# Two-layer encoder trunk: pools laid out anew, first weights ahead of the parameters, layer 1's loads spread over each head, layer 1's head outputs kept in SBUF

## The chip, the core and the metric

The kernel runs on one core of a Trainium2 chip. The metric is the device time of one launch in microseconds. The engines are PE (TensorE, matmuls), DVE (VectorE), ACT (ScalarE), POOL (GpSimd) and SP (SyncE), which here issues every DMA in one queue, in order.

## The reference

The input is x, 2048 tokens by 1024, in float32. There are two layers:

```
layer 0: h = rms_norm(x); proj = h @ W_in          (1024 x 3328)
  mixer A: 8 query heads on 2 KV heads, rotary, window of 3 chunks of 64, a learned sink
  mixer B: 8 heads, own chunk + 8 before, relative-position bias
  x1 = x + concat(A * silu(gate_a), B * silu(gate_b)) @ W_out
layer 1: h = rms_norm(x1); proj = h @ W_in         (1024 x 4096)
  mixer C, 8 heads: a = softmax(q1 k1) - lam * softmax(q2 k2), causal by chunk of 64
  o = rms_norm(a @ v) * (1 - lambda_init)
  out = x1 + (o * silu(gate)) @ W_out
```

## The kernel before

All matmul operands are split into a high and a low part (`...H`, `...L`), and a product is three matmuls (hi·hi and two cross terms, `mm3`, L214 to L216). The tokens are four blocks (b = 0 to 3) of 512, each four tiles (j) of 128. There are four stages, one after the other:

- **p0** (`_project`, layer 0). `hidden(b)` loads four x tiles (`xt`), normalizes them and transposes them into `p0h`. `weights` loads a group of columns in four pieces of 512 KB (`ws`, L297), splits each into `wH` (ACT copy, L303) and `wL` (POOL subtraction, L304). Each group is multiplied with two blocks of tokens. `tables()` loads the small parameters, multiplies out the rotary tables, and comes between the two blocks of `hidden`.
- **m** (`_mix0`): both attention mixers of layer 0 and its output projection (`mom`). `qd` holds a head's high query part (three buffers), `ql` the low part (two buffers).
- **p1** (`_project`, layer 1), in two halves of two blocks: the q, k and v columns, written to DRAM.
- **c** (`_mix1`): mixer C. Heads run block by block from b = 3 down to 0, eight heads to a block. `scores(h, b)` works through j and, in each j, through the two maps m and the key chunks z of 512: two matmuls into `cS` (L878, L879), row maximum on DVE (`cnm`, L882), exponential on ACT (`cP`, L885). `values(h, b)` transposes the weights (`ctr`, L925), splits them into `cptH` (ACT) and `cptL` (DVE), and multiplies them with v into `cO` (L932 to L934). `side()` brings other matmul work between: the gates of all blocks (`cG`, 288 steps, weights `cwH`, `cwL`) and then the output projections (`com`).

The order of the work in c is set by `pace`, which lets the values trail the scores by `LAG1` units and takes as many side steps as the table `STAGES1` gives for the units done. Instructions are then put on the engines by a scheduler that simulates the program; on the chip each engine, and SP's queue of DMAs, runs its list in order. A tile waits until the tile that had its buffer is done with, and the first tiles of a new stage's pool wait for what lay at that place in the stage before: pools are stacked in the order in which they are made.

In c before the change, `load(h, i, K, V)` loads for head h and key chunk i the four pieces of K (L1002, L1003) and then V (L1009), all ahead of the head's scores, and q after that (L859, L860). A head's output `o` is gated in `rest()`; for b = 1 and 2 it is stored to a DRAM tensor `o`, and `fetch(b)` reads it back later and splits it into `y` for the output projection.

Of the kernel before, what the change touches and what calls it, by code (L numbers as in the profile page):

```python
# [85 lines left out]
class Trunk:  # L86
# [6 lines left out]
    STAGES1 = ((0, 0), (600, 288), (780, 360), (1000, 440), (1088, 520))  # L93
# [130 lines left out]
    def _project(self, es, layer):  # L224
# [68 lines left out]
        def weights(c0, width, W=W):  # L293
            wH, wL = [], []
            for kh in range(4):
                ws = st.tile([P, 2, 512], F32, tag="ws", name=n + "ws")
                nc.sync.dma_start(  # L297
                    ws[:, :, :width],
                    W[kh * 256:(kh + 1) * 256, c0:c0 + width].rearrange("(k p) c -> p k c", p=P),
                )  # L300
                for k in range(2):
                    h, l = weight_tiles()
                    nc.scalar.activation(h[:, :width], ws[:, k, :width], AF.Copy)  # L303
                    nc.gpsimd.tensor_tensor(l[:, :width], ws[:, k, :width], f32(h[:, :width]), ALU.subtract)  # L304
                    wH.append(h)
                    wL.append(l)
            return wH, wL

        def hidden(b):
            hH, hL = hidden_tile("H", b), hidden_tile("L", b)  # L310
            for j in range(NTB):
# [8 lines left out]
                for q in range(2):  # L320
# [8 lines left out]
                    nc.vector.tensor_tensor(oL, ps3, f32(oH), ALU.subtract)  # L329
            if layer == 1 and b < NB - 1:  # L330
# [78 lines left out]
        for half in range(2):  # L409
            blocks = (2 * half, 2 * half + 1)  # L410
            h = [hidden(blocks[0])]
# [4 lines left out]
            for gi, (kind, c0, width, o) in enumerate(groups):  # L416
                w = weights(c0, width)
# [87 lines left out]
    def _mix0(self, es):  # L505
# [18 lines left out]
        def load_q(H, L, h, b, res):  # L524
# [6 lines left out]
            ql = ld.tile([P, BLK], F32R, tag="ql", name=n + "ql")  # L531
# [203 lines left out]
        def projected(b):  # L735
# [3 lines left out]
            for j, c in units:  # L739
# [87 lines left out]
    def _mix1(self, es):  # L827
        nc, tc, a, s = self.nc, self.tc, self.a, self.s1
        n = "c"
        pool = lambda nm, bufs, **kw: es.enter_context(tc.tile_pool(name=n + nm, bufs=bufs, **kw))  # L830
        ot = pool("ot", 4)
        sm = pool("sm", 8)
        ld = pool("ld", 2)
        yp = pool("y", 2 * KT)
        vp = pool("v", 4)
        pp = pool("pp", 19)
        kp = pool("kp", 4)
        sb = pool("sb", 2)
# [12 lines left out]
        def scores(h, b, K, res):  # L851

            tok = slice(b * BLK, (b + 1) * BLK)
            qd = ld.tile([P, 2, BLK], F32R, tag="qd", name=n + "qd")
            ql = ld.tile([P, 2, BLK], F32R, tag="ql", name=n + "ql")
            for m in range(2):
                r = slice(m * HD, (m + 1) * HD)
                for part, q in (("qH", qd), ("qL", ql)):
                    nc.sync.dma_start(f32(q[0:HD, m, :]), s[part][h, r, tok])  # L859
                    nc.sync.dma_start(f32(q[HD:P, m, :]), s[part][h, r, tok])  # L860
            us = res["u"] = []
            for j in range(NTB):
# [9 lines left out]
                for m in range(2):  # L872
                    chunks = []
                    for z, (c, ce) in enumerate(cuts):
                        wd = ce - c
                        ps = pS.tile([P, 512], F32, tag="S", name=n + "S")[:, :wd]
                        kt = K[z][m]
# [5 lines left out]
                        chunks.append((sb if m else pp).tile([P, 512], F32, tag=f"P{m}", name=n + f"P{m}", bufs=6 if m else None))  # L883
                        acc = la[:, m, z:z + 1] if nb > 1 else l[:, m:m + 1]
                        nc.scalar.activation(chunks[z][:, :wd], ps, AF.Exp, bias=nm[:, m, z:z + 1], accum_out=acc)  # L885
                        yield wd / 256
# [28 lines left out]
        def values(h, b, V, res):  # L915
# [3 lines left out]
            for kt in range(nkt):  # L919
# [6 lines left out]
                H = sb.tile([P, 512], F32R, tag="ptH", name=n + "ptH", bufs=3)  # L926
                L = sb.tile([P, 512], F32R, tag="ptL", name=n + "ptL", bufs=3)
# [3 lines left out]
                vH, vL = (v[:, kk:kk + P] for v in V[kt // 4])  # L931
                mm(o, vH, H[:, :wd], start=(kt == 0), stop=False, skip_group_check=True)  # L932
                mm(o, vH, L[:, :wd], start=False, stop=False, skip_group_check=True)  # L933
                mm(o, vL, H[:, :wd], start=False, stop=(kt == nkt - 1), skip_group_check=True)  # L934
# [8 lines left out]
        def gate(h, b, O):  # L943

            rows, tok = slice(h * P, (h + 1) * P), slice(b * BLK, (b + 1) * BLK)
            g = sb.tile([P, BLK], F32, tag="g", name=n + "gg")
# [10 lines left out]
            def rest():  # L957
# [10 lines left out]
                ended.add((h, b))  # L968
# [3 lines left out]
        def y_tile(b):  # L972
            if b:
                return yp.tile([P, BLK], F32R, tag="y", name=n + "y")
            pl, tag = late.pop(0)
            return pl.tile([P, BLK], F32R, tag=tag, name=n + "y" + tag, bufs=3 if pl is ld else None)

        def split(h, b, o):
            yH, yL = y_tile(b), y_tile(b)
            nc.scalar.activation(yH, o, AF.Copy)  # L980
            nc.gpsimd.tensor_tensor(yL, o, f32(yH), ALU.subtract)
            y[b][h] = yH, yL

        def fetch(b):

            for h in range(8):
                while (h, b) not in ended:
                    yield 0
                if b < NB - 1:
                    o = ot.tile([P, BLK], F32, tag="ot", name=n + "oy")  # L990
                    nc.sync.dma_start(o, s["o"][h * P:(h + 1) * P, b * BLK:(b + 1) * BLK])
                    split(h, b, o)
                    yield 1

        def load(h, i, K, V):

            tok = slice(i * BLK, (i + 1) * BLK)
            ks = []
            for m in range(2):
                k = kp.tile([P, BLK], F32R, tag=f"k{m}", name=n + f"k{m}")  # L1000
                r, o = slice(m * HD, (m + 1) * HD), slice((1 - m) * HD, (2 - m) * HD)
                nc.sync.dma_start(f32(k[r, :]), s["kH"][h, r, tok])  # L1002
                nc.sync.dma_start(f32(k[o, :]), s["kL"][h, r, tok])  # L1003
                ks.append(k)
            K.append(ks)
# [7 lines left out]
            V.append(vs)  # L1013

        room = self.last_hidden
        ended = set()
        late = [(ld, "wH"), (ld, "wL")] * 3 + [(kp, "k0"), (kp, "k1"), (vp, "vH"), (vp, "vL")] * 2 + [(pp, "P0")] * 2
# [5 lines left out]
        def gates():  # L1023

            for b in reversed(range(NB)):
                tok = slice(b * BLK, (b + 1) * BLK)
                for c in range(8):
                    ps = pG.tile([P, BLK], F32, tag="G", name=n + "G")
                    for k in range(KT):
                        if k % 4 == 0:  # L1030
                            w = []
                            for part in "HL":
                                t = ld.tile([P, 4, P], F32R, tag="w" + part, name=n + "w" + part, bufs=3)
# [47 lines left out]
        def projected_last():  # L1081

            w = [(room[0][:, k, :], room[1][:, k, :]) for k in range(KT)], []
            tags = [(ld, "qd"), (ld, "ql")] * 2, [(sb, "P1")] * 6 + [(kp, "k0"), (kp, "k1")]
# [4 lines left out]
            for i in range(4):  # L1089
                pairs.append([  # L1090
                    pl.tile([P, BLK], F32R, tag=tag, name=n + "w" + tag, bufs=6 if tag == "P1" else None)
# [4 lines left out]
            for c, w in ((1, w[0]), (0, pairs)):  # L1096
                tiles = [out_begin(0, j, c) for j in range(NTB)]
                for k in range(KT):
                    while (k, 0) not in ended:
                        yield 0  # L1100
# [9 lines left out]
        def heads():  # L1110
            for b in reversed(range(NB)):
                at[0] = b
                for h in range(8):
                    K, V = [], []
                    for i in range(b + 1):
                        load(h, i, K, V)
                    res = {}
                    yield from scores(h, b, K, res)
                    queue.append(values(h, b, V, res))
            queue.append(leave())  # L1120
# [6 lines left out]
        def side():  # L1127
            yield from gates()
            for b in (3, 2, 1):
                yield from fetch(b)  # L1130
# [51 lines left out]
```

## Time and profile before

| | |
|---|---|
| median of three runs | 2928.43 us (2926.35 to 2938.07) |
| profiled execution: time, span | 2935.29 us, 2933.5 us |
| mean granted TensorE clock | 0.972 |
| PE, DVE, ACT, POOL busy | 2726.8, 1937.4, 1595.9, 1610.5 us |
| moved by DMA | 555.83 MB, mean 189 GB/s |
| stages (first matmuls of each) | p0 from 0, m from about 610, p1 from about 1204, c from 1804 us |

The granted clock is told in shares of the full rate. PE is busy 93% of the span, so its idle time is 206 us in all; where an engine waits, the profile names what it waited for last.

### The profile page before, as it was taken

Reading aid. Unit: us, or ns where it says so; the run is one execution under the profiler, and the core shown is the slowest. Engines: PE = TensorE matmul, PEld = TensorE weight load, DVE = VectorE, ACT = ScalarE, POOL = GpSimd, SP = SyncE. Lnnn points to the kernel's source line nnn. Section 1 sums busy time; section 2 is a strip of 40 time slices with the busy share of each in tenths; the row PEclk is TensorE's granted clock in tenths of the full one; section 3 lists DMA queues with packets and bytes.
Section 4 is the critical chain, followed back from the end, with each engine's and each line's share of the span. In section 5 each row is a group of like instructions: output and inputs, shape, how many; then the busy total and the mean of one; then the engine's idle time right before and its main releaser. Section 6 shows DMA issues by size and latency. Waiting matters only on the chain.

```text
span 2933.5 us, 45206 instructions
## 1 busy us (share of the span) xinstructions
PE 2726.8 (93%) x13704; PEld 2243.6 (76%) x13704; DVE 1937.4 (66%) x4685; ACT 1595.9 (54%) x4135; POOL 1610.5 (55%) x1968
## 2 busy tenths in 40 slices
PE   7999999998999999999999997889999999898898
PEld 5878888886887887777888885767777777677667
DVE  7752385256788885698548832656657888888742
ACT  4443543367676664334343322657657777777752
POOL 3541251246344443367646631767767778888851
PEclk9999999999999999999999998999999999999999
DMA  4673343649887764567884454585867777668863
GB/s 149 224 249 128 116 144 122 196 145 245 218 205 172 191 176 123 193 209 258 271 288 129 130 176 148 165 233 164 248 180 217 203 226 216 181 182 220 209 216 115
DMA packets 408866, 555.83 MB, mean 189 GB/s; under 512 B 47152, under 2 KB 187184, under 8 KB 408624
## 3 DMA queue, kind: packets, MB, share of 16 engines
q1 hardware_dynamic: 408624, 552.96, 64.1%
q8 instruction: 109, 1.79, 0.3%
q14 instruction: 133, 1.09, 0.1%
HBM read 388.18 MB, written 164.63 MB: 188 GB/s over the span
## 4 chain that ended last, share of the span: by engine, by line
PE 64%; DMA 11%; DVE 11%; ACT 4%; issue 2%; POOL 2%; SPq 1%; DVEq 0%; ACTq 0%; POOLq 0%
PE p1mm L216 4%; PE p1mm L214 4%; PE p1mm L215 4%; PE cS L878 3%; PE cS L879 3%; PE ctr L925 3%; PE p0mm L214 2%; PE p0mm L215 2%; PE p0mm L216 2%; PE cG L214 2%; PE cG L215 2%; PE cG L216 2%; PE cO L933 2%; PE mom L214 2%; PE com L214 2%
## 5 line engine op out<-in xcount | busy, mean ns | idle before, releaser
L885 ACT ACTIVATE cP<-cS,cnm 128x512 f32<-128x512 f32 (+3 forms) x640 | 398.4, 629 | 183.0 <-DVE cnm L882 104.3
L882 DVE TENSOR_REDUCE cnm<-cS 128x1 f32<-128x512 f32 (+3 forms) x640 | 373.6, 600 | 105.9 <-PE cS L879 100.6
L878 PE MATMUL cS<-ck,cqd 128*128 128x512 f32 (+3 forms) x640 | 265.7, 420 | 56.4 <-ACT cP L885 19.7
L304 POOL TENSOR_TENSOR p0wL<-p0ws,p0wH 128x512 fp32r<-128x512 f32 (+1 forms) x128 | 155.5, 1246 | 274.3 <-ACT p0wH L303 264.9
L214 PE MATMUL p1mm<-p1wH,p1hH 128*128 128x512 f32 x768 | 301.8, 394 | 0.8 <-ACT p1wH L303 0.8
L215 PE MATMUL p1mm<-p1wL,p1hH 128*128 128x512 f32 x768 | 301.8, 393 | 0.4 <-POOL p1wL L304 0.4
L216 PE MATMUL p1mm<-p1wH,p1hL 128*128 128x512 f32 x768 | 301.9, 394 | 0.0
L912 POOL TENSOR_TENSOR cP<-cP,cP 128x512 f32<-128x512 f32 (+3 forms) x256 | 284.7, 1132 | 0.4
L304 POOL TENSOR_TENSOR p1wL<-p1ws,p1wH 128x512 fp32r<-128x512 f32 x128 | 167.9, 1331 | 137.1 <-ACT p1wH L303 117.6
L214 PE MATMUL p0mm<-p0wH,p0hH 128*128 128x512 f32 (+1 forms) x640 | 238.1, 375 | 3.4 <-ACT p0vt L454 2.9
L879 PE MATMUL cS<-ck,cql 128*128 128x512 f32 (+3 forms) x640 | 238.1, 377 | 2.9 <-DMA cql<-qL 2.9
L216 PE MATMUL p0mm<-p0wH,p0hL 128*128 128x512 f32 (+1 forms) x640 | 238.2, 373 | 0.1
L215 PE MATMUL p0mm<-p0wL,p0hH 128*128 128x512 f32 (+1 forms) x640 | 238.2, 373 | 0.0
L929 DVE TENSOR_TENSOR cptL<-ctr,cptH 128x512 fp32r<-128x512 f32 (+1 forms) x320 | 190.5, 599 | 62.9 <-ACT cptH L928 62.1
L928 ACT ACTIVATE cptH<-ctr 128x512 fp32r<-128x512 f32 (+1 forms) x320 | 169.9, 539 | 64.8 <-PE ctr L925 63.5
L878 PEld LDWEIGHTS cS<-ck,cqd 128*128 128x128 f32 x640 | 124.6, 195 | 98.4 <-ACT cP L885 45.7
L906 POOL TENSOR_SCALAR cP<-cP,ccs 128x512 f32<-128x512 f32 (+3 forms) x288 | 188.9, 672 | 0.0
L925 PE MATMUL ctr<-ident,cP 128*128 128x128 f32 x1088 | 175.5, 277 | 0.6 <-POOL cP L912 0.3
L898 POOL TENSOR_SCALAR ccs<-ce,crl 128x4 f32<-128x4 f32 (+2 forms) x96 | 26.9, 280 | 270.1 <-ACT cP L885 130.1
L911 POOL TENSOR_SCALAR cP<-cP,ccs 128x512 f32<-128x512 f32 (+3 forms) x256 | 173.6, 691 | 0.0
L215 PEld LDWEIGHTS p1mm<-p1wL,p1hH 128*128 128x128 f32 x768 | 144.8, 189 | 29.8 <-POOL p1wL L304 0.8
L214 PEld LDWEIGHTS p1mm<-p1wH,p1hH 128*128 128x128 f32 x768 | 144.7, 189 | 29.7 <-ACT p1wH L303 1.0
(325 smaller groups left out, 7873.8 us busy)
## 6 DMA issues: line engine op xcount, KB each, us to landing
p1ws<-in_od_w_in_dram SPq DMA_DIRECT2D x56, 512.0 KB, 4.8
p0ws<-in_ev_w_in_dram SPq DMA_DIRECT2D x48, 512.0 KB, 4.2
ck<-kH SPq DMA_DIRECT2D x160, 128.0 KB, 4.0
ck<-kL SPq DMA_DIRECT2D x160, 128.0 KB, 4.2
cvH<-vH SPq DMA_DIRECT2D x80, 256.0 KB, 3.8
cvL<-vL SPq DMA_DIRECT2D x80, 256.0 KB, 4.5
cqd<-qH SPq DMA_DIRECT2D x128, 128.0 KB, 4.9
cql<-qL SPq DMA_DIRECT2D x128, 128.0 KB, 4.8
```

The source lines that it names most:

```text
L214: mm(ps, aH, bH, start=first, stop=False)
L215: mm(ps, aH, bL, start=False, stop=False)
L216: mm(ps, aL, bH, start=False, stop=last)
L304: nc.gpsimd.tensor_tensor(l[:, :width], ws[:, k, :width], f32(h[:, :width]), ALU.subtract)
L878: mm(ps, qd[:, m, js], kt[:, :wd], start=True, stop=False)
L879: self.anchor = mm(ps, ql[:, m, js], kt[:, :wd], start=False, stop=True).ins
L882: nc.vector.tensor_reduce(nm[:, m, z:z + 1], ps, AX.X, ALU.max, negate=True)
L885: nc.scalar.activation(chunks[z][:, :wd], ps, AF.Exp, bias=nm[:, m, z:z + 1], accum_out=acc)
L906: nc.gpsimd.tensor_scalar(p1, p1, c1, 1.0, ALU.mult, ALU.mult)
L912: nc.gpsimd.tensor_tensor(p1, p1, p2, ALU.add)
L925: nc.tensor.transpose(tp[:, (j - j0) * P:(j - j0 + 1) * P], us[j][kt // 4][:, kk:kk + P], self.ident)
L929: nc.vector.tensor_tensor(L[:, :wd], tp[:, :wd], f32(H[:, :wd]), ALU.subtract)
```

## The change

The diff, cut to what the prediction speaks of:

```diff
-    STAGES1 = ((0, 0), (600, 288), (780, 360), (1000, 440), (1088, 520))
+    STAGES1 = ((0, 0), (32, 45), (600, 288), (830, 360), (1035, 432), (1088, 490))
 # _project: pools
         if layer == 1:
             ev = pool("ev", 2)
-            wp = pool("w", 28)
-            gp = pool("g", 2)
         sb = pool("sb", 2)
         sm = pool("sm", 4)
-        tb = pool("tab", 1)
+        if layer == 1:
+            gp = pool("g", 2)
         st = pool("st", 3 - layer)
         xp = pool("x", 3)
+        if layer == 1:
+            wp = pool("w", 28)
+        tb = pool("tab", 1)
 # weights, now a generator; first=True for group 0 of the first half
-                    nc.gpsimd.tensor_tensor(l[:, :width], ws[:, k, :width], f32(h[:, :width]), ALU.subtract)
+                    low = nc.vector if first and k else nc.gpsimd
+                    low.tensor_tensor(l[:, :width], ws[:, k, :width], f32(h[:, :width]), ALU.subtract)
 # first half: a piece of weights, then x tile and piece in turn
+                by = weights_by(groups[0][1], groups[0][2], W, *ready, first=True)
+                next(by)
+                h = [hidden(blocks[0], by)]
 # _mix0
-            ql = ld.tile([P, BLK], F32R, tag="ql", name=n + "ql")
+            ql = ld.tile([P, BLK], F32R, tag="ql", name=n + "ql", bufs=3)
-            for j, c in units:
+            for j, c in units if b < NB - 1 else units[NTB:] + units[:NTB]:
 # _mix1: pools, in the order of their places
-        ot(4) sm(8) ld(2) y(16) v(4) pp(19) kp(4) sb(2)
+        y(16) q(2) kp(4) v(4) p2(6) pp(19) sb(3) w(3) ot(4) sm(8)
 # values
-                mm(o, vH, L[:, :wd], start=False, stop=False, skip_group_check=True)
-                mm(o, vL, H[:, :wd], start=False, stop=(kt == nkt - 1), skip_group_check=True)
+                mm(o, vL, H[:, :wd], start=False, stop=False, skip_group_check=True)
+                mm(o, vH, L[:, :wd], start=False, stop=(kt == nkt - 1), skip_group_check=True)
 # rest(): the store to DRAM and fetch() are gone, every head splits at once
-                if b in (0, NB - 1):
-                    split(h, b, o)
-                else:
-                    nc.sync.dma_start(s["o"][rows, tok], o)
+                yH, yL = y_tile(h, b), y_tile(h, b)
+                nc.scalar.activation(yH, o, AF.Copy)
+                nc.gpsimd.tensor_tensor(yL, o, f32(yH), ALU.subtract)
+        late = [(kp, "k0"), (kp, "k1"), (vp, "vH"), (vp, "vL")] + [(wp, "wH"), (wp, "wL")] * 3
+        homes = {
+            3: [(yp, "y")] * 16, 2: late + [(yp, "y")] * 6,
+            1: [(yp, "y")] * 10 + late[:4] + [(pp, "P0")] * 2, 0: [(yp, "y")] * 6 + late,
+        }
 # heads(): called after each score step (j, m, z) of a head; nxt is the next head
+                def then(j, m, z):
+                    if (j, m, z) == (2, 0, 0) and nxt:
+                        after[0] = load_q(*nxt)
+                    if j == NTB - 1:
+                        if nxt and z <= nxt[1]:
+                            after[1][z, m] = load_k(nxt[0], z, m)
+                        if m == 0:
+                            res["v"].append(load_v(h, z))
```

The two lines of pools of `_mix1` are written short here, with the buffers in brackets. So q of the next head is asked for in j = 2, each K piece of the next head as soon as the last score on that piece is issued (in j = 3), and V of the head itself in j = 3.

The numbers in the names are those of buffers. The first place is SP's queue at the start of the program (stage p0). `p0g_in` is the norm's gain, `p0xt` an x tile, `p0ws` a piece of weights, the others are small parameters. Before:

```order
L314 DMA p0xt_207<-in_x_dram 128x1024
L159 DMA ev_a_q_norm_100<-in_ev_a_q_norm_dram 128x64
L159 DMA ev_a_k_norm_101<-in_ev_a_k_norm_dram 128x64
L159 DMA od_q_norm_102<-in_od_q_norm_dram 128x64
L159 DMA od_k_norm_103<-in_od_k_norm_dram 128x64
L162 DMA bq_g_104<-in_ev_b_q_norm_dram 64x1
L163 DMA bk_g_105<-in_ev_b_k_norm_dram 64x1
L162 DMA bq_g_104<-in_ev_b_q_norm_dram 64x1
L163 DMA bk_g_105<-in_ev_b_k_norm_dram 64x1
L165 DMA sink_107<-in_ev_a_sinks_dram 128x8
L173 DMA sub_110<-in_od_subln_dram 128x1
L297 DMA p0ws_437<-in_ev_w_in_dram 128x2x512
```

After:

```order
L263 DMA p0g_in_141<-in_ev_norm_dram 128x1024
L304 DMA p0ws_143<-in_ev_w_in_dram 128x2x512
L323 DMA p0xt_155<-in_x_dram 128x1024
L304 DMA p0ws_186<-in_ev_w_in_dram 128x2x512
L323 DMA p0xt_196<-in_x_dram 128x1024
L304 DMA p0ws_227<-in_ev_w_in_dram 128x2x512
L323 DMA p0xt_237<-in_x_dram 128x1024
L159 DMA ev_a_q_norm_100<-in_ev_a_q_norm_dram 128x64
```

Three pieces of weights have moved ahead of ten small loads and stand between the x tiles.

The second place is SP's queue where p1 ends and c begins; the stores `<-p1vH` and `<-p1vL` are p1's last. Before, all of K of the first head is loaded further up:

```order
L1009 DMA cvH_20918<-vH_74 128x4x128
L1009 DMA cvL_20920<-vL_75 128x4x128
L467 DMA vH_74<-p1vH_20860 128x512
L468 DMA vL_75<-p1vL_20861 128x512
L1009 DMA cvH_20928<-vH_74 128x4x128
L1009 DMA cvL_20930<-vL_75 128x4x128
L1009 DMA cvH_20938<-vH_74 128x4x128
L1009 DMA cvL_20940<-vL_75 128x4x128
L1009 DMA cvH_20948<-vH_74 128x4x128
L1009 DMA cvL_20950<-vL_75 128x4x128
L859 DMA cqd_20952<-qH_70 64x512
L860 DMA cqd_20952<-qH_70 64x512
```

After, q of the first two heads is loaded further up:

```order
L1046 DMA cwH_20964<-wgH_82 128x512
L1046 DMA cwL_20966<-wgL_83 128x512
L487 DMA vH_74<-p1vH_20860 128x512
L488 DMA vL_75<-p1vL_20861 128x512
L1046 DMA cwH_20992<-wgH_82 128x512
L1046 DMA cwL_20994<-wgL_83 128x512
L1046 DMA cwH_21044<-wgH_82 128x512
L1046 DMA cwL_21046<-wgL_83 128x512
L1014 DMA ck0_20928<-kH_72 64x512
L1015 DMA ck0_20928<-kL_73 64x512
L1014 DMA ck0_20931<-kH_72 64x512
L1015 DMA ck0_20931<-kL_73 64x512
```

V and q no longer stand between p1's last stores and the first scores; the gates' weights and K do. The first K tiles now lie on a pool of p1 with its `vH` and `vL` in it, and their load waits until p1's last two stores have landed.

The third place is PE at the same point, after p1's last matmul. Before:

```order
L216 MATMUL p1mm_20835<-p1wH_20614,p1hL_18149 128x512
L878 MATMUL cS_20967<-ck0_20912,cqd_20952 128x512
L878 MATMUL cS_20981<-ck0_20922,cqd_20952 128x512
L878 MATMUL cS_20987<-ck0_20932,cqd_20952 128x512
L878 MATMUL cS_20996<-ck0_20942,cqd_20952 128x128
L879 MATMUL cS_20967<-ck0_20912,cql_20953 128x512
L879 MATMUL cS_20981<-ck0_20922,cql_20953 128x512
L879 MATMUL cS_20987<-ck0_20932,cql_20953 128x512
L879 MATMUL cS_20996<-ck0_20942,cql_20953 128x128
L214 MATMUL cG_20973<-p1hH_18148,cwH_20974 128x512
L215 MATMUL cG_20973<-p1hL_18149,cwH_20974 128x512
L216 MATMUL cG_20973<-p1hH_18148,cwL_20976 128x512
```

After:

```order
L216 MATMUL p1mm_20835<-p1wH_20614,p1hL_18149 128x512
L905 MATMUL cS_20957<-ck0_20928,cqd_20918 128x512
L906 MATMUL cS_20957<-ck0_20928,cql_20919 128x512
L214 MATMUL cG_20963<-p1hH_18148,cwH_20964 128x512
L215 MATMUL cG_20963<-p1hL_18149,cwH_20964 128x512
L216 MATMUL cG_20963<-p1hH_18148,cwL_20966 128x512
L214 MATMUL cG_20963<-p1hH_18148,cwH_20964 128x512
L215 MATMUL cG_20963<-p1hL_18149,cwH_20964 128x512
L216 MATMUL cG_20963<-p1hH_18148,cwL_20966 128x512
L905 MATMUL cS_20974<-ck0_20931,cqd_20918 128x512
L906 MATMUL cS_20974<-ck0_20931,cql_20919 128x512
L214 MATMUL cG_20963<-p1hH_18148,cwH_20964 128x512
```

Before, eight score matmuls on four K pieces come first; now a pair of score matmuls on one K piece alternates with one or two gate steps of three matmuls.

More of the change, by code (lines that the diff above doesn't have):

```diff
@@ L329, in hidden @@
                     nc.vector.tensor_tensor(oL, ps3, f32(oH), ALU.subtract)
+                next(between, None)
+            for _ in between:
+                pass
             if layer == 1 and b < NB - 1:
@@ L978, in split @@
[L978 to L993, printed above, removed]
@@ L1098, in projected_last @@
                 for k in range(KT):
-                    while (k, 0) not in ended:
+                    while k not in y[0]:
                         yield 0
@@ L1110, in heads @@
         def heads():
-            for b in reversed(range(NB)):
+            order = [(h, b) for b in reversed(range(NB)) for h in range(8)]
+            q, K = load_q(*order[0]), {(i, m): load_k(0, i, m) for m in range(2) for i in range(NB)}
+            for (h, b), nxt in zip(order, order[1:] + [None]):
                 at[0] = b
[L1113 to L1119, printed above, removed]
+                after, res = [None, {}], {"v": []}
+                def then(j, m, z):
[6 more added lines that the diff above has]
+                            res["v"].append(load_v(h, z))
+                yield from scores(h, b, q, K, res, then)
+                queue.append(values(h, b, res))
+                q, K = after
             queue.append(leave())
```

98 lines of the change are left out of this document (55 added, 43 removed).

## The prediction

> **What bounds the kernel.** I read the page's engine rows first, then PE's busy time and clock stage by stage, then PE's waits, then single moments in the order of time.
>
> ```profile
> PE 2726.8 (93%) x13704; PEld 2243.6 (76%) x13704; DVE 1937.4 (66%) x4685; ACT 1595.9 (54%) x4135; POOL 1610.5 (55%) x1968
> PE 64%; DMA 11%; DVE 11%; ACT 4%; issue 2%; POOL 2%; SPq 1%; DVEq 0%; ACTq 0%; POOLq 0%
> ```
>
> PE is busy 93% of the span and holds 64% of the chain that ended last; DMA and DVE hold 11% each. The change takes away no matmul, so the time can only come from PE's idle time, 2933.5 - 2726.8 = 206.7 us, and from matmuls run at a lower clock. The next rows give both by stage; the columns are the stretch, then busy time of PE, PEld, DVE, ACT, POOL, then the granted clock, the DMA share and GB/s.
>
> ```profile
> 0.00:100.00 100.00, 75.98 (x412) 64.95 (x412) 77.27 (x166) 45.47 (x113) 47.17 (x45) 0.97 0.48 154
> 640.00:800.00 160.00, 140.03 (x847) 121.92 (x847) 114.52 (x434) 112.52 (x305) 84.81 (x134) 0.97 0.86 231
> 800.00:1157.00 357.00, 332.76 (x2052) 291.04 (x2051) 278.21 (x922) 231.09 (x601) 158.16 (x228) 0.98 0.67 170
> 1157.00:1250.00 93.00, 83.92 (x375) 67.72 (x374) 57.64 (x108) 34.09 (x80) 32.19 (x24) 0.95 0.59 199
> 1790.00:1860.00 70.00, 45.88 (x166) 33.26 (x165) 34.09 (x72) 30.39 (x89) 35.80 (x50) 0.80 0.68 192
> 1860.00:2200.00 340.00, 315.68 (x1514) 252.80 (x1514) 214.32 (x470) 219.13 (x597) 234.40 (x309) 0.95 0.69 197
> 2200.00:2600.00 400.00, 373.25 (x1844) 294.30 (x1844) 327.49 (x720) 293.40 (x825) 323.86 (x446) 0.98 0.72 203
> 2600.00:2780.00 180.00, 159.99 (x801) 128.64 (x801) 148.75 (x394) 134.49 (x395) 152.03 (x234) 0.96 0.82 216
> ```
>
> PE idles 24.0 us in the first 100, 44.2 in stage m (640 to 1157), 9.1 at the border to p1, 24.1 in the first 70 us of stage c, 24.3, 26.8 and 20.0 in the rest of it shown here. The clock's loss is (1 - clock) times the stretch: 14 us in 1790 to 1860, 17 in 1860 to 2200, 12 in stage m. Who PE waits for (total, times, longest):
>
> ```profile
> PE cO L933 <- DVE cptL L929: 22.3, 21, 3.9
> PE cS L878 <- ACT cP L885: 19.7, 34, 4.6
> PE cS L878 <- DMA cql<-qL: 14.6, 2, 13.3
> PE mSA L568 <- DMA mql<-aqL: 12.5, 6, 3.6
> PE cS L878 <- DMA ck<-kL: 8.5, 5, 4.6
> PE cS L878 <- DMA cvH<-vH: 7.6, 1, 7.6
> PE p0trh L324 <- DVE p0xt L319: 6.0, 2, 4.6
> PE p0trh L324 <- DVE p0q8r L208: 5.6, 1, 5.6
> PE mSB L568 <- DMA mql<-bqL: 4.2, 4, 2.2
> PE mom L214 <- DVE mxr L486: 4.0, 1, 4.0
> ```
>
> **The change, part by part.** The sum goes against the profiled execution, 2935.29 us (span 2933.5 and 1.8 around it); it stands 6.9 us above the median of 2928.43, so a gain is taken off that median.
>
> *Start.* The ten small loads leave the place ahead of the weights.
>
> ```profile
> 6.34 1.06 ACT L317 ACTIVATE p0junk<-p0xt 128x1024 f32<-128x1024 f32 x1 [4.01 <-DMA p0xt<-in_x_dram]
> 9.32 1.04 ACT L317 ACTIVATE p0junk<-p0xt 128x1024 f32<-128x1024 f32 x1
> 10.63 1.69 SPq L297 DMA_DIRECT2D p0ws<-in_ev_w_in_dram  x3
> 18.21 0.78 PE L214 MATMUL p0mm<-p0wH,p0hH 128*128 128x512 f32 x1
> ```
>
> The weights were issued at 10.63 and the first product came at 18.21. Now a piece of weights comes where the first x tile was (in use at 6.34), and the x tile one place later; blocks of 512 KB follow each other by about 1.5 us there (6.34 to 9.32 is two), so the first product can come near 14, 4 us earlier. But the third x tile is now the seventh block instead of the fourth, 4 to 5 us later, and the 5.6 us wait for `p0q8r` is for DVE, which is busy 77 of the first 100 us with norms and tables and gets four weight subtractions more (a 128x512 one takes 0.68 us here, below). Gain 3 us; ends: 2.7 lost (four times 0.68) and 11.6 gained (both waits, 6.0 + 5.6).
>
> ```profile
> 32.26 0.68 DVE L186 TENSOR_TENSOR p0tqC<-p0cos,ev_a_q_norm 128x512 f32<-128x512 f32 x1
> 33.46 1.23 DVE L186 TENSOR_TENSOR p0tkC<-p0cos,ev_a_k_norm 128x512 f32<-128x512 f32 x1
> 32.91 2.38 POOL L304 TENSOR_TENSOR p0wL<-p0ws,p0wH 128x256 fp32r<-128x256 f32 x2 [2.26 <-ACT p0wH L303]
> ```
>
> The same DVE operation takes 0.68 us alone and 1.23 us while POOL subtracts. The Trainium skill has a rule against halving this work between the two (SBUF — State Buffer, SBUF: two separate sides): DVE and GpSimd share a port pair that one holds for a whole instruction while the other blocks. By that rule the four subtractions cost 4.9 us of DVE instead of 2.7 and the start gains about 1 instead of 3. The trace agrees in kind.
>
> *Stage m, a third `ql`.* PE waits 12.5 + 4.2 = 16.7 us for `ql`, which is the later of a head's two query parts; `qd`, with three buffers, is never in the list. With three, `ql` can be issued beside `qd`. The transfers stay, and at DMA share 0.86 in 640 to 800 (10.2 of the 12.5 us lie there) some are late whatever their issue; K and bias, next in SP's queue, become the last to land. I take 11 of the 16.7 and 2 of the clock's 12. Ends: 0 and 28.
>
> *Border to p1.* The split weights of p1 move out from under layer 0's output tiles, so two groups can be loaded and split (16 ACT copies, 16 POOL subtractions) beside the last projection; there POOL stands idle:
>
> ```profile
> 1207.52 2.53 POOL L304 TENSOR_TENSOR p1wL<-p1ws,p1wH 128x512 fp32r<-128x512 f32 x2 [48.17 <-ACT p1wH L303]
> ```
>
> But PE is idle only 9.1 us in 1157 to 1250, of which 4.0 is for `mxr` behind p1's loads in SP's queue, and those loads become more. Gain 3; ends -4 (that wait once more) and 9. The other order of the last block's halves moves no work: 0, since all of its weights are loaded by then.
>
> *Border to c.*
>
> ```profile
> 1790.06 0.39 PE L215 MATMUL p1mm<-p1wL,p1hH 128*128 128x512 f32 x1
> 1790.28 0.39 PE L216 MATMUL p1mm<-p1wH,p1hL 128*128 128x512 f32 x1
> 1792.30 0.38 SPq L468 DMA_DIRECT2D vL<-p1vL  x1
> 1804.00 1.73 PE L878 MATMUL cS<-ck,cqd 128*128 128x512 f32 x4 [13.33 <-DMA cql<-qL]
> 1834.38 0.59 SPq L1003 DMA_DIRECT2D ck<-kL  x1
> ```
>
> The median landing times of the loads and stores in question, from the list of DMA issues:
>
> ```profile
> ck<-kL SPq DMA_DIRECT2D x160, 128.0 KB, 4.2
> vL<-p1vL SPq DMA_DIRECT2D x32, 256.0 KB, 4.0
> ```
>
> The gap stays: K now waits for the last store, issued at 1792.30 and landed 4.0 later, then two issues of 0.59 and a landing of 4.2: first scores near 1801.7, 2.3 us earlier than 1804.00. After it, K pieces come every 1.2 us and find a score pair and one or two gate steps between them, and 45 gate steps in the first 32 units instead of 15. So of the other 11 us idle up to 1860 I take 5, and 3 of the clock's 14. Gain 10; ends -5 (gates' loads ahead of K) and 38 (all of it).
>
> The Trainium skill (TensorE: Matmul & The Clock Gate, Part 1: The HAM clock gate) says that PE's clock halves after an idle window of about 3.4 us and needs as long of work to come back, however much longer the gap was. By that rule a gap of 11 us costs the same low stretch as one of 13.3, and the 3 us of clock here would be 0. The trace agrees that a gap is followed by a low clock (0.80 here, the lowest row).
>
> *Loads inside c.* Waits there for K, V and q are 8.5 + 7.6 + 1.3 (14.6 less the border's) = 17.4 us. V waited in SP's queue for the head before to finish, with K and q behind it:
>
> ```profile
> SPq L1009 <- PE cO L934: 70.4, 30, 7.7
> SPq L1002 <- PE cS L879: 51.1, 46, 6.9
> ```
>
> Asked for in j = 3, V finds its buffers free; q is asked for half a head ahead. K still waits for the last score on its buffer (the 51.1). I take 9 of 17.4 and 3 of 17 of clock: 12. Ends: 34 and the loss of the third rival.
>
> *Order of the value matmuls.* `cptL` is now used one 512-column matmul later (0.22 us from start to start, 1790.06 to 1790.28 above): 21 waits x 0.22 = 4.6; take 4, ends 0 and 5.
>
> *Outputs kept.* 32 DMAs of 256 KB and their issues go (32 x 0.4 = 13 us of SP, hidden under PE); the splits stay. Against it, block 2's last three heads wait for `y` buffers until block 3's projection is done, each holding one of four `ot` buffers. Gain 1; ends -10 and 5. The later steps of `STAGES1` only shift projection steps: behind the last head PE's list has 129 `com` matmuls instead of 108, so 21 x 0.22 = 4.6 us of work move from under the heads to the tail; 0 while the heads keep PE as full as before, 5 lost if not.
>
> Sum: 3 + 13 + 3 + 10 + 12 + 4 + 1 = 46 us. 2928.4 - 46 = 2882 us, 1.6% faster.
>
> **The rivals.**
> *Moved waits in c.* The loads come late again for another reason, since SP issues 16 K pieces (0.59 us each) and 8 V loads in the last quarter of a head, about 14 us: border 2 instead of 10, loads 0 instead of 12. Sum 26: 2902. For it: the longest K wait, 4.6, was behind K alone.
> *No clock back.* The gaps shrink but all remain, and with each its stretch at a low clock, as the 0.80 behind the 13.3 us gap; the clock's terms, 2 + 3 + 3, go: 2890. The rule of the Trainium skill's page on the clock, above, would do this.
> *All of it.* The waits aimed at vanish with their clock: 10 + 24 + 9 + 24 + 24 + 5 = 96: 2832.
> *No change.* Transfers, not their issue, set `ql`, and DVE the start: only 5 remain: 2923.
> *Slower.* K, V and q crowd at the end of each of the 24 heads of blocks 3, 2 and 1, and PE waits at every border as it did at worst for K, 4.6 us. 24 x 4.6 = 110 less the 46 would be far slower; it decides from 46 / 24 = 1.9 us a border. I price it at 2.8: 67 - 46 = 21 slower, 2949. Against it: these loads only move, and PE's list puts eight score steps between a K piece's release and its next use.
>
> **How the numbers follow.** Forecast 0.50, its own range 2866 to 2898; moved waits 0.18; no clock 0.08; all of it 0.08; no change 0.07; slower 0.09. 0.5% (14.6 us, to 2913.8) is about what a measurement of this kernel can tell from no change. Faster: 0.50 + 0.08 + 0.08 and two thirds of 0.18 = 0.78; same: the rest of that and no change, 0.13; slower 0.09. From 2842 to 2922 the range leaves out the slower case, most of no change and half of all of it, under 0.2.
>
> **What would show it.** Right: first `p0mm` near 14; no wait for `mql` over 2 us; first `cS` 11 to 12 us after p1's last matmul, clock over 0.85 in the 70 us behind it; no wait of PE for `cvH`; `cptL` waits under 19 us. Wrong: waits for `ck` of more than 2 us a head, ACT's split waiting for `com`, or stage c no shorter than 1130 us from its first score.

## The result and the profile after

The changed kernel takes 2912.08 us (median of 10 runs) against 2932.01 us for the kernel before (10 runs beside it): ratio 0.9933, 95% interval 0.9911 to 0.9955, some 20 us faster. The forecast was 46 us. The profiled execution of after has a span of 2911.2 us, 22.3 below that of before. Below are its engine row, its stretches (busy time of PE, PEld, DVE, ACT, POOL, then clock, DMA share and GB/s), three stretches of before that hold the same work as 559 to 612, 806 to 1122 and 1206 to 1310 here, and its waits of PE:

```profile
PE 2715.5 (93%) x13704; PEld 2239.9 (77%) x13704; DVE 1937.6 (67%) x4693; ACT 1593.2 (55%) x4135; POOL 1599.2 (55%) x1960
```

```profile
0.00:100.00 100.00, 79.00 (x437) 66.60 (x438) 82.11 (x185) 48.77 (x123) 43.71 (x46) 0.97 0.51 161
559.00:612.00 53.00, 44.24 (x196) 36.31 (x194) 6.41 (x10) 19.65 (x32) 10.94 (x11) 0.95 0.30 95
646.00:806.00 160.00, 144.00 (x855) 123.36 (x854) 122.14 (x442) 113.95 (x311) 87.55 (x139) 0.95 0.85 231
806.00:1122.00 316.00, 295.36 (x1849) 258.56 (x1848) 259.06 (x888) 214.81 (x567) 144.70 (x216) 0.98 0.73 183
1206.00:1310.00 104.00, 94.67 (x460) 78.43 (x459) 87.61 (x187) 48.77 (x119) 43.07 (x34) 0.95 0.56 192
1796.00:1866.00 70.00, 57.91 (x253) 46.13 (x252) 34.80 (x76) 34.83 (x99) 36.35 (x50) 0.93 0.81 245
1866.00:2200.00 334.00, 314.74 (x1520) 251.19 (x1519) 226.61 (x490) 227.30 (x620) 246.56 (x326) 0.96 0.72 202
2200.00:2600.00 400.00, 370.13 (x1847) 295.45 (x1846) 337.18 (x741) 292.92 (x835) 332.41 (x462) 0.98 0.69 189
```

Before:

```profile
561.00:605.00 44.00, 44.00 (x196) 36.44 (x195) 5.54 (x8) 17.95 (x29) 9.31 (x8) 1.00 0.25 83
800.00:1118.00 318.00, 295.31 (x1843) 259.06 (x1842) 261.43 (x886) 213.59 (x565) 144.26 (x216) 0.98 0.72 181
1203.00:1300.00 97.00, 89.94 (x442) 73.03 (x441) 89.58 (x167) 48.21 (x117) 62.57 (x46) 1.00 0.68 236
```

After, waits of PE (total, times, longest):

```profile
PE cS L905 <- DMA ck<-kL: 29.9, 18, 3.3
PE cO L962 <- DVE cptL L957: 15.0, 17, 3.4
PE cS L905 <- DMA ck<-kH: 10.9, 1, 10.9
PE mSA L587 <- DMA mvA<-av: 9.3, 1, 9.3
PE p1trh L333 <- DVE p1xt L328: 8.6, 1, 8.6
PE mSA L587 <- DMA mqd<-aqH: 5.7, 2, 3.5
PE mSA L587 <- ACT mPA L642: 5.5, 6, 1.5
PE mSB L587 <- ACT mPA L642: 4.6, 2, 2.5
PE mSA L588 <- DMA mql<-aqL: 3.1, 2, 1.9
```

The waits that the change aimed at are gone or smaller (`ql` 16.7 to 3.1 us, `cvH` 7.6 to none). Three are new, 9.3 us for `mvA`, 8.6 us for p1's first normed tile and 5.7 us for `mqd`, the high query part of stage m; in that stage the waits for ACT's `mPA` rose from 4.2 to 10.1 us, and those for K inside stage c from 8.5 to 29.9. How the 22.3 us come about is seen best in the places where one stage follows another. This table is worked out from the first and last matmuls of `p0mm`, `p0mg`, `mSA`, `mSB`, `mom`, `p1mm` and `cS` in the two traces; PE's idle time stands behind the length.

| from, to | before, idle | after, idle | gained |
|---|---|---|---|
| start and layer 0's projection | 605.8, 32.7 | 603.3, 28.4 | 2.5 |
| last gate product to first score of m | -0.2 | 9.3, 9.3 | -9.5 |
| stage m to its last score | 512.4, 45.1 | 509.4, 39.2 | 3.0 |
| its last projection | 85.6, 5.6 | 85.1, 7.2 | 0.5 |
| to p1's first product | 3.9, 0.9 | 10.4, 8.6 | -6.5 |
| p1 | 583.2, 13.3 | 579.7, 7.7 | 3.5 |
| to the first score of c | 13.3, 13.3 | 10.9, 10.9 | 2.4 |
| stage c to its last score | 1059.0, 87.1 | 1033.7, 80.0 | 25.3 |
| the rest | 70.6, 8.8 | 69.5, 4.4 | 1.1 |

From p1's end on it gave 28.8 us and at the start 2.5, close to the forecast; stage m gave 3 instead of 13, and 16 us were lost at the two borders ahead of m and p1.

### The profile page after: what moved, and what is told of

The parts are those of the page before. It is cut to its first block, busy times and chain, and to the rows that moved or that the text cites. A ratio compares the mean times of both kernels' runs of the same rounds, so it can differ in the third digit from the quotient of the medians.

```text
span 2911.2 us, 45153 instructions
## 1 busy us (share of the span) xinstructions
PE 2715.5 (93%) x13704; PEld 2239.9 (77%) x13704; DVE 1937.6 (67%) x4693; ACT 1593.2 (55%) x4135; POOL 1599.2 (55%) x1960
## 5 line engine op out<-in xcount | busy, mean ns | idle before, releaser
L905 PE MATMUL cS<-ck,cqd 128*128 128x512 f32 (+3 forms) x640 | 263.3, 413 | 62.9 <-DMA ck<-kL 29.9
L312 POOL TENSOR_TENSOR p0wL<-p0ws,p0wH 128x512 fp32r<-128x512 f32 (+1 forms) x124 | 149.3, 1234 | 306.1 <-ACT p0wH L310 295.7
L312 POOL TENSOR_TENSOR p1wL<-p1ws,p1wH 128x512 fp32r<-128x512 f32 x124 | 160.9, 1316 | 105.6 <-ACT p1wH L310 101.1
L956 ACT ACTIVATE cptH<-ctr 128x512 fp32r<-128x512 f32 (+1 forms) x320 | 169.8, 541 | 69.5 <-PE ctr L953 68.4
L215 PEld LDWEIGHTS p1mm<-p1wL,p1hH 128*128 128x128 f32 x768 | 145.0, 189 | 28.8
L216 PEld LDWEIGHTS p1mm<-p1wH,p1hL 128*128 128x128 f32 x768 | 144.7, 188 | 29.0
```

The costliest lines, as they stand in the source:

```text
L215: mm(ps, aH, bL, start=False, stop=False)
L216: mm(ps, aL, bH, start=False, stop=last)
L312: low.tensor_tensor(l[:, :width], ws[:, k, :width], f32(h[:, :width]), ALU.subtract)
L905: mm(ps, qd[:, m, js], kt[:, :wd], start=True, stop=False)
```

## The experiments

Each ratio is to the kernel before, run beside it on the same chip. Stage lengths and waits are those of one profiled execution. The code is cut to the lines that matter.

**ql3_only.** The kernel before, and

```
- ql = ld.tile([P, BLK], F32R, tag="ql", name=n + "ql")
+ ql = ld.tile([P, BLK], F32R, tag="ql", name=n + "ql", bufs=3)
```

> The kernel before with one edit, the third ql buffer of stage m. In the changed kernel stage m is 3.0 us shorter from its first score to its last than before (509.4 against 512.4 us), and its first score comes 9.3 us after layer 0's last gate product instead of at once. Theory (pools): those 9.3 us are not ql's, they come from the rotary tables' pool of layer 0, which now lies behind the weight staging; so here the first score follows at once, and stage m shows what ql alone is worth: 500 us by the forecast's term of 13, total 2916. Rival 1 (ql pushes): the third buffer moves the loads behind it 2 KB up and that makes them late: gap of 9 us here too. Rival 2 (transfers): the transfers set ql, stage m stays within 3 us of 512, total 2925 to 2930.

Measured: 0.9996 (0.9982 to 1.0011), nothing. The first score of m follows at once, so the 9.3 us are not ql's. Stage m takes 517.9 us. Of its waits of PE, and of SP's and POOL's rows:

```profile
PE mom L216 <- POOL myL L594: 7.2, 1, 7.2
PE mSA L567 <- ACT mPA L622: 6.8, 7, 1.4
PE mSA L568 <- DMA mql<-aqL: 2.2, 2, 1.3
```

```profile
747.13 0.63 SPq L681 DMA_DIRECT2D mbias<-in_relb_dram  x1
...
756.02 0.48 POOL L682 TENSOR_SCALAR mbias<-mbias,mfar 128x256 f32<-128x256 f32 x1 [8.28 <-DMA mbias<-in_relb_dram]
756.47 1.26 POOL L594 TENSOR_TENSOR myL<-myt,myH 128x512 fp32r<-128x512 f32 x1
```

The waits for `ql` went, and none of it came out at the end: PE's idle time in stage m was 46.2 us, against 45.1 before. The largest of the waits that came in their place is this one: POOL stood 8.28 us for a bias tile, with the split that the projection needed queued behind it, and PE 7.2 us for that. The others are small ones, as for `mPA` (4.2 before, 8.3 here).

**tab_back.** The changed kernel, and

```
  sm = pool("sm", 4)
+ if layer == 0:
+     tb = pool("tab", 1)
  ...
- tb = pool("tab", 1)
+ if layer == 1:
+     tb = pool("tab", 1)
```

> The changed kernel with the pool of layer 0's rotary tables back ahead of the weight staging (layer 1's pools stay changed). Theory (pools): in the changed kernel stage m's load tiles lie on the weight staging, which is in use to the end of layer 0's projection, so all of stage m's first loads stand behind the gate stores in SP's queue; here they stand 65 us earlier, as before. The first score of stage m follows the last gate product within 1 us instead of 9.3, and the total falls by 9 to 12 us, to about 2901. Rival (ql pushes): no change, 2912.

Measured: 0.9869 (0.9843 to 0.9894), and no gap ahead of stage m. Against the changed kernel that is some 19 us, more than the 9 to 12 expected; stage m itself takes 501.5 us instead of 509.4. SP's rows of the changed kernel and of this one:

```profile
567.98 34.25 SPq L457 DMA_DIRECT2D g<-p0gt  x7
604.12 0.33 SPq L568 DMA_DIRECT2D mfar<-in_relfar_dram  x1
608.67 0.59 SPq L578 DMA_DIRECT2D mvA<-av  x1
```

```profile
538.67 0.59 SPq L580 DMA_DIRECT2D mvA<-av  x1
567.85 34.25 SPq L459 DMA_DIRECT2D g<-p0gt  x7
```

The changed kernel issues m's first loads behind seven gate stores, 70 us later than this one. By the addresses in the built programs m's load pool (139.9 to 179.7 KB in each partition) reaches into the weight staging (170.5 to 182.5 KB) in the changed kernel; in this one, as before, the staging begins at 186.5 KB, behind the pool's end. The tiles that m loads first, `mvA` among them, lie from 141.4 to 159.7 KB, clear of the staging in both. So the pool waited as a whole, and not just the tiles that overlap.

**tab_sm_back.** tab_back, and

```
- sm = pool("sm", 4)
  if layer == 1:
      gp = pool("g", 2)
+ sm = pool("sm", 4)
```

> As the last one, and p1's pool of small sums (sm) behind the pool g instead of ahead of it, so that it no longer lies on layer 0's last output tiles. Theory (pools): in the changed kernel the first norm of p1 waits 11.5 us, to the landing of layer 0's last output store, and PE 8.6 us for it; here p1's norms run beside the last projection as before, the first transposes follow the last product within 1 us, and the total falls by a further 8 us, to about 2893. Rival 1 (queue): the norm is late because the x tiles stand behind p1's weights in SP's queue; then the gap stays at 8 to 9 us. Rival 2 (given back): p1 starts earlier but then waits for weights, and its end comes no more than 3 us earlier.

Measured: 0.9842 (0.9821 to 0.9862). p1's first norm (ACT) and first transposes (PE) in the changed kernel, and the first norm here:

```profile
1211.12 1.06 ACT L326 ACTIVATE p1junk<-p1xt 128x1024 f32<-128x1024 f32 x1 [11.53 <-DMA x<-mxr]
```

```profile
1206.65 0.39 PE L216 MATMUL mom<-mw,myL 128*128 128x512 f32 x1
1215.68 1.55 PE L333 MATMUL p1trh<-ident,p1xt 128*128 128x128 f32 x6 [8.64 <-DVE p1xt L328]
```

```profile
1162.56 1.07 ACT L328 ACTIVATE p1junk<-p1xt 128x1024 f32<-128x1024 f32 x1
```

The first norm runs 33 us ahead of the last projection's end instead of 4 behind it, with the sums out of layer 0's pool `y`, and from the last projection's end to p1's first product it is 0.9 us instead of 10.4. That pool holds layer 0's output tiles (`mxr`, from 114.4 KB), whose store the wait names; by their addresses the sums (112.4 to 113.9 KB) lay beside these tiles, so again a whole pool was waited for. The interval overlaps tab_back's, so the time alone does not settle it; the trace shows the wait gone.

**tab_sm_two_ql.** tab_sm_back, and

```
- ql = ld.tile([P, BLK], F32R, tag="ql", name=n + "ql", bufs=3)
+ ql = ld.tile([P, BLK], F32R, tag="ql", name=n + "ql")
```

> The last kernel with two ql buffers again. Read against it this gives what the third buffer is worth once stage m starts on time. By the forecast's term stage m gets 13 us longer (2906); if transfers set ql whatever its buffers, no more than 3 us (2894 to 2896). If the third buffer only shifts the wait to K and bias, the waits for mql fall and those for the K tiles rise by as much.

Measured: 0.9900 (0.9878 to 0.9923), so here the third buffer is worth 0.6%, and stage m is 517.1 us against 507.1: the forecast's size, in a kernel where no bias wait takes it back. The waits for `ql`, 1.9 us in tab_sm_back, are here:

```profile
PE mSA L590 <- DMA mql<-aqL: 10.6, 8, 4.3
PE mSB L590 <- DMA mql<-bqL: 10.1, 7, 3.1
```

Of the two profiled executions the spans are alike (2897.1 and 2896.6), since this one had the shorter stage c; the times decide.

**ql3_bias_first.** ql3_only, with the bias load of `scores_b` moved ahead of its K load:

```
  load_q("bqH", "bqL", h, b, res)
+ bias = ld.tile([P, 256], F32, tag="bias", name=n + "bias")
+ nc.sync.dma_start(bias, a["relb"][h])
  ks = load_k(...
```

> The kernel before with the third ql buffer (0.9996) and one more edit: a head's bias is asked for ahead of its K and V in stage m. In ql3_only the waits for ql went (16.7 to 2.2 us and less), but POOL stood 8.3 us for a bias tile, and PE 7.2 us for POOL at a step of the projection. Theory (bias): that one wait ate the gain; with the bias early it goes and stage m comes 8 to 12 us shorter (517.9 to 506 to 510 us), ratio 0.996 to 0.997. Rival 1 (another wait follows): stage m stays at 512 to 518, since ACT's and DVE's chains (6.8 us of waits for mPA, 8.2 for mptL) end next. Rival 2 (transfers): the waits for ql come back, since the bias takes their place in the queue.

Measured: 0.9954 (0.9938 to 0.9969), 12 us below ql3_only, with stage m at 506.3 us.

```profile
PE mom L216 <- POOL myL L594: 3.7, 1, 3.7
PE mSA L568 <- DMA mql<-aqL: 1.8, 2, 1.4
```

PE's wait for the split halves, those for `ql` stay away, and the idle time in stage m falls from 46.2 to 37.7 us. This fits that in ql3_only the late bias had taken back the third buffer's gain. But no run has the early bias without the third buffer, so what it is worth alone is not shown; in the kernel before PE does not wait for that split at all.

**loads_only.** The kernel before with the new `load_q`, `load_k`, `load_v` and `heads` and nothing else; of its edit, the place where a head's loads stood:

```
- for i in range(b + 1):
-     load(h, i, K, V)
- yield from scores(h, b, K, res)
+ yield from scores(h, b, q, K, res, then)
```

> The kernel before with one edit: in stage c, q is asked for half a head ahead, a head's K pieces in the last quarter of the head before, and V in its own last quarter, as in the changed kernel; stage c's pools, the outputs' way through memory, the order of the value products and the steps of the gates are as before. By the forecast's term the loads inside c are worth 12 us with the border's 13.3 us gap left: 0.996. If head_loads (35 us above its kernel) is the measure, 0.990. If the moved loads only pay with the other steps of the gates (45 steps in the first 32 units), 0.999 to 1.0.

Measured: 0.9928 (0.9907 to 0.9950), 21 us: as much as the whole change. From p1's last product to the first score it is 3.9 us, shorter than in the changed kernel:

```profile
1787.52 0.39 PE L216 MATMUL p1mm<-p1wH,p1hL 128*128 128x512 f32 x1
1791.78 1.21 PE L881 MATMUL cS<-ck,cqd 128*128 128x512 f32 x4 [3.87 <-issue]
```

**head_loads.** tab_sm_back, and in `heads`, with a `then` that does nothing:

```
- q, K = load_q(*order[0]), {(i, m): load_k(0, i, m) for m in range(2) for i in range(NB)}
- for (h, b), nxt in zip(order, order[1:] + [None]):
+ for h, b in order:
+     res = {"v": []}
+     K = {}
+     for i in range(b + 1):
+         K.update({(i, m): load_k(h, i, m) for m in range(2)})
+         res["v"].append(load_v(h, i))
+     q = load_q(h, b)
```

> Edit: stage c's loads as the kernel before has them: K and V of a head and then its q asked for at the head's first score, nothing ahead; pools, value order and kept outputs stay changed. By the forecast's terms the loads inside c are worth 12 us and the border to c up to 10: total 12 to 22 us higher than 0.9842 of before (0.988 to 0.992). If the moved loads give nothing because the waits only moved (the forecast's rival), the total stays at 0.984.

Measured: 0.9962 (0.9945 to 0.9979), 1.2% above tab_sm_back (35 us, where 12 to 22 were expected); from p1's last product to the end it takes 1143.9 us, as before (1142.9). Without the moved loads the new pools of c, the value order and the kept outputs together gain nothing from there on.

**c_border.** tab_sm_back with stage c's pools in another order (written short, their sizes unchanged):

```
- yp, qp, kp, vp, pq, pp, sb, wp, ot, sm
+ yp, kp, wp, sm, vp, pq, pp, sb, ot, qp
```

> From here on the kernel compared with is the one with the pools tab and sm put right (0.9842 of before, profiled span 2896.6 us, 11.6 us from p1's last product to stage c's first score, 26.8 us of waits for K inside stage c). Edit: stage c's pools in another order, so that K and the gate weights lie on p1's work tiles (sb) and q on p1's rotary tables, both done long before p1 ends, and no longer on p1's store tiles (g). Theory (pools): K and q are issued ahead of p1's last eight stores instead of behind them, the first score comes 2 to 4 us after the last product, and with the clock kept behind so short a gap the total falls by 8 to 15 us. Rival 1: something else is as late (PSUM of the last products, the memory of the first probabilities, which lies on p1's weights): the gap falls by no more than 3 us. Rival 2: K's 16 transfers ahead of the last stores delay these, and V, q or gate weights behind them cost it again: gap short, total the same.

Measured: 0.9818 (0.9794 to 0.9843); the interval overlaps tab_sm_back's. The border in the changed kernel (SP's issues, then PE), and here (PE, then the 70 us behind it):

```profile
1798.59 0.38 SPq L488 DMA_DIRECT2D vL<-p1vL  x1
1802.73 0.45 SPq L1014 DMA_DIRECT2D ck<-kH  x1
```

```profile
1796.77 0.39 PE L216 MATMUL p1mm<-p1wH,p1hL 128*128 128x512 f32 x1
1808.08 0.77 PE L905 MATMUL cS<-ck,cqd 128*128 128x512 f32 x1 [10.91 <-DMA ck<-kH]
```

```profile
1780.78 0.39 PE L216 MATMUL p1mm<-p1wH,p1hL 128*128 128x512 f32 x1
1781.00 0.39 PE L907 MATMUL cS<-ck,cqd 128*128 128x512 f32 x1
1780.00:1850.00 70.00, 66.45 (x295) 53.10 (x294) 38.30 (x88) 40.31 (x114) 40.07 (x58) 0.98 0.69 211
```

The gap is gone and the clock behind it is 0.98. So the 10.9 us in the changed kernel are its own pools'. The first K tile does not itself lie on p1's store tiles: it is at 98.4 KB, and only the end of K's pool (114.4 KB) reaches 0.5 KB into the pool of `vH` and `vL` (from 113.9 KB). The whole pool of K waited here too.

**k_first.** tab_sm_back, and in `then`

```
+ early = nxt and b + nxt[1] <= 2
- if (j, m, z) == (2, 0, 0) and nxt:
+ if nxt and (j, m, z) == (0 if early else 2, 0, 0):
      after[0] = load_q(*nxt)
+ if early and (j, m, z) == (1, 0, 0):
+     after[1].update({(i, e): load_k(nxt[0], i, e) for e in range(2) for i in range(nxt[1] + 1)})
  if j == NTB - 1:
-     if nxt and z <= nxt[1]:
+     if nxt and not early and z <= nxt[1]:
          after[1][z, m] = load_k(nxt[0], z, m)
-     if m == 0:
-         res["v"].append(load_v(h, z))
+     if (m, z) == (1, b):
+         res["v"] += [load_v(h, i) for i in range(b + 1)]
```

> Edit: within a head's last quarter all K pieces of the next head are asked for ahead of V's (V once, behind the last K piece), and in blocks 1 and 0, where the four K buffers hold this head's and the next head's pieces together, K is asked for after the head's first quarter and q at its start. Theory (SP's queue): the 26.8 us of waits for K inside stage c come from K standing behind V's waits for the values of the head before and behind hidden tiles' reloads; they fall to under 12, those in blocks 1 and 0 nearly to none, total 8 to 15 us lower. Rival 1 (last score): K waits for the release of its own buffer by the last scores, so only the waits in blocks 1 and 0 fall (10 us or less). Rival 2: V is now late and PE waits for cvH or cvL at the first value product of a head; total unchanged.

Measured: 0.9788 (0.9756 to 0.9819), 16 us below tab_sm_back. PE's waits for K, of which the first row is the border:

```profile
PE cS L907 <- DMA ck<-kH: 11.0, 1, 11.0
PE cS L907 <- DMA ck<-kL: 11.0, 7, 2.5
```

Inside c the waits for K fall from 27 us to 11. By block, 3 to 0, they were 9.5, 7.3, 3.0 and 7.7 in tab_sm_back and are 8.0, 1.3, 1.5 and 0.3 here. In blocks 3 and 2, where only V has moved behind K, block 2 loses its waits and block 3 keeps them; in the short blocks, where K is also asked for earlier, they go. Stage c is 27.9 us shorter from its first to its last score, and the rest behind it 12.9 us longer, so part of the gain is paid back in the tail.

**old_values.** tab_sm_back with the old order again:

```
- mm(o, vL, H[:, :wd], start=False, stop=False, skip_group_check=True)
- mm(o, vH, L[:, :wd], start=False, stop=(kt == nkt - 1), skip_group_check=True)
+ mm(o, vH, L[:, :wd], start=False, stop=False, skip_group_check=True)
+ mm(o, vL, H[:, :wd], start=False, stop=(kt == nkt - 1), skip_group_check=True)
```

> Edit: the order of the value products as the kernel before has it, vH by ptL ahead of vL by ptH. The forecast's term: PE's waits for ptL go up from 22.6 us in 17 waits (this kernel's profile) by 17 times 0.22 = 3.7 us and the total by 4; ends 0 and 5. Against the term: over the four profiles with the new order these waits are 13.0 to 22.6 us in 17 each, over the two with the old order 22.3 and 27.0 in 21 and 23, so the spread is as large as the term.

Measured: 0.9859 (0.9829 to 0.9888), with 16.9 us in 18 waits for `ptL`, inside the spread of the new order. Inconclusive.

**border_k_first** is the edits of c_border and k_first together; **best_bias_first** adds the early bias.

> The edits of c_border (0.9818) and k_first (0.9788) together, on the kernel with both pools put right (0.9842). If they are independent, as their places are (the first 15 us of stage c, and the head borders), the ratio is 0.976 to 0.977, about 2862 us, with a gap of under 1 us at the border and under 13 us of waits for K inside c. If SP's queue is what both live from, the gain of one is lost: 0.979.

> border_k_first with the bias early in stage m as well. In that family stage m is 501 to 508 us with no bias wait over 2.4 us, so by the theory of ql3_bias_first there is little left: within 3 us of border_k_first. If bias loads delay others by chance of the order, stage m would be shorter by 5 us or more.

Measured: 0.9793 (0.9770 to 0.9815) and 0.9778 (0.9757 to 0.9799), 2868.29 us for the latter, the lowest ratio of all, 2.2% below the kernel before and 1.6% below the changed one. The two traces have no gap at the border, and the first has 10.9 us of waits for K; still neither ratio is below k_first's by more than the intervals allow. Why the border adds nothing measurable on top of k_first stays open.

## Why the prediction was right and wrong

Its direction and its range held; its size did not: 20 us of 46. The step that failed is its account of the moved pools. Only for K's pool in stage c did it ask what lies on the new place. For layer 0's table pool the sum has no term, and at p1's pool of sums it did not look. In the runs with these two pools put back the time falls to 0.9869 and 0.9842 of the kernel before, some 19 and 27 us below the changed kernel's 0.9933, and the forecast, 2882 of 2928.4, was 0.984.

*Start*, 3 forecast: 2.5; the first product came at 14.5, where about 14 was forecast.

*Third `ql`*, 13 forecast: stage m gave 3.0. The waits for `ql` went as said (none over 1.9 us is left), but others came: PE's idle time in the stage fell by 5.9 us only, and its loss by the clock rose from 13.7 to 17.5 us. With the table pool put back the size was about right: in the eight kernels that have it so, and three buffers, stage m is 501.5 to 507.9 us, in the three kernels with two (before, loads_only and tab_sm_two_ql) 512.2 to 517.1. The step named what would be late next ("K and bias, next in SP's queue, become the last to land") and gave it no price. With the buffer alone (ql3_only) the new waits took the whole gain, and with the bias early as well the time is 12 us lower. In the changed kernel no wait of PE for that split is in the trace, so there the bias is not shown to be the cause.

*A term that was missing*: the sum has none for layer 0's table pool, which the diff moves behind the weight staging. It cost 9.5 us ahead of stage m, and stage m was 1.5 to 7.9 us longer than in those eight kernels.

*Border to p1*, +3 forecast with -4 as the low end: -3.0 in all. p1 itself was 3.5 us shorter, which the early weights may have given (no run has them alone), but the term looked at POOL and at `mxr`, and never at what `sm` now lies on; that cost 6.5. With `sm` moved the border and p1 are 587.1 - 582.3 = 4.8 us shorter than before. The sum was near for a change with pools in the right places, and this one had two in the wrong ones. That it is so near is partly luck: the profiled execution of tab_sm_back, the longest of its four runs, has a span only 36.9 us below that of before.

*Border to c, loads, value order, outputs*, 27 together: 28.8. That is partly luck of the parts. The gap came as worked out (11 to 12 us said, 10.9 idle), and the clock behind it came back further: 0.93 instead of 0.80 in 70 us is 9 us, where the sum had 3 and the rival by the clock rule none. But loads_only gives 21 us without any new pool, with a gap of 3.9: q ahead of V shortens the border by itself, and the new place of K takes most of that back. So the moved loads carry the gain (loads_only, head_loads). Value order and kept outputs were not resolved: the one is within the spread, the other was not tried alone.

*The slower rival* was right in kind: K does come late, 18 times, 29.9 us, always in the first six score steps of a head, at 14 of the 31 borders between heads. That is 1.0 us a border, against the 1.9 from which it would have decided. Mending it gave 16 us (k_first). In loads_only, with the same order of loads, the waits for K inside c come to 14.0 us, so other parts of the change add to them; which was not separated.

## What to carry to other kernels

Moving a pool moves the first instruction of the stage that later lies there: for every pool that a diff moves, list the pools whose range it touches in the stage before and after it, and when the last tile of these is done with, down to a 1.5 KB pool of sums. In all three cases here the first tiles of the new pool lay clear of the tiles that were waited for. When a wait is taken off a queue, price the next entry of that queue and who stands behind its consumer. Loads asked for just in time should go in the order in which they are needed first (K ahead of V), and earlier wherever buffers are free.

## What the hardware showed that was not expected

In loads_only gaps of 3.9 and 2.2 us at the border to c were followed by a half-clock stretch of 10.2 us, as long as that behind the changed kernel's one gap of 10.9 us; without a gap (c_border) the only one in those 70 us was 3.4 us long. The Trainium skill (TensorE: Matmul & The Clock Gate, Part 1: The HAM clock gate) says that the clock halves after an idle window of about 3.4 us; that a short gap brought as long a stretch as a long one agrees. The stretch is not always the same: it was 13.7 us at the gap of 11.6 in tab_sm_back and 17.1 at the 13.3 of the kernel before. Part of each lies in the gap itself; counted from the first score it lasted 3.3 us in the changed kernel, 6.0 and 8.0 in those two. And the clock records show 29 half-clock stretches in the kernel before with only 14 gaps of PE of 3.4 us or more, and 30 in c_border with two, so shorter gaps cost clock as well. In ql3_only the waits for `ql` fell from ten to two, and one of 7.2 us and several small ones came in their place; the idle time in stage m hardly changed (45.1 to 46.2 us), and its loss by the clock rose from 13.7 us to 18.8 (the length of each low stretch times what is lacking to full clock).

The landing time of a load varies: the bias tile that POOL waited for was issued at 747.13 and used at 756.02, 8.9 us, where K's median landing in the same run was 4.2 us. The DMA share was 1.08 from 747 to 756 us and 0.70 in stage c from 1810 to 2600; that this is the reason is not shown.
